# One unused 4-byte tile among the constants: every tile that grows from the bottom of SBUF moves up by 32 bytes

## The chip, the core and the metric

The kernel runs on one core of a Trainium2 chip. The metric is the device time of one execution in microseconds, as the median of several runs. The core has a matrix engine (TensorE, PE in the profile), three engines for elementwise work (VectorE or DVE, ScalarE or ACT, GpSimd or POOL) and a queue that issues transfers (SyncE, SP). Tiles live in SBUF, 128 partitions with a row of bytes each; an address here is the offset in that row. PE takes two operands from SBUF, the weights (stationary, loaded first) and the moving operand (streamed through), and writes its sums to PSUM.

## What is computed

A decoder trunk of two layers on 1024 tokens with 1024 channels, all in float32:

```python
for i in range(DEPTH):                       # DEPTH = 2
    mod = c_act @ ada_w[i] + ada_b[i]
    sh1, sc1, g1, sh2, sc2, g2 = [m[:, None, :] for m in jnp.split(mod, 6, axis=-1)]
    h = _rmsnorm(x, norm1_g[i]) * (1.0 + sc1) + sh1
    if i % N_MIXERS == 0:
        y = _dsa_mixer(h, positions, ...)    # indexer, top 256 keys, attention, w_out
    else:
        y = _short_conv_mixer(h, ...)        # conv_w_in, 3-tap convolution, conv_w_out
    x = x + g1 * y
    h = _rmsnorm(x, norm2_g[i]) * (1.0 + sc2) + sh2
    x = x + g2 * _swiglu(h, ffn_w_gate[i], ffn_w_up[i], ffn_w_down[i])   # hidden 2816
```

## The kernel before

**How products are formed.** Every large product is split in three: an operand x becomes hi = x rounded to the matrix engine's fp32r format and lo = x - hi, and `mm3` (line 510) issues three matmuls, hi x hi, hi x lo, lo x hi, into one PSUM bank. `split` (line 506) makes hi with ScalarE (a cast, or a copy on VectorE) and lo with VectorE. The call is `mm(ps, weights, moving)`: the second argument is the stationary operand, the third the moving one, 128 rows by 512 tokens in most of the program.

**Stages.** Norm and projections of the attention (to about 300 us), indexer and attention (to about 660 us), then the part that class `Tail` writes: FFN of layer 0 in `Pair` objects (lines 1772 to 1845), its down projection in `down_pairs` (line 1548), the convolution layer, again in `Pair` objects, its output product in `down` (line 1506), FFN and down projection of layer 1. A `Pair` and `down_pairs` use Strassen's scheme (Winograd's form): seven products in place of eight, and sums on VectorE around them.

**Who reads what.** In a `Pair` the weights come from the ring `whi`/`wlo` (four buffers each, `unit` at line 528) and the moving operands are the resident tiles `h11`, `h21`, `h22`, `t1` to `t4` (line 1405). In `down_pairs` five of the seven products move the tile `ph11` and two (`m2`, `m4`, lines 1659 and 1666) move buffers of the `whi`/`wlo` ring; the weights come from the ring in all seven. In `down` the first half of the tokens moves ring buffers, the second half the resident tiles `rh22` and `rt1`. The attention's projections move `hhi`/`hlo`. The profile leaves the numbers out of names: `h` stands for h11, h21 and h22, `t` for t1 to t4, `ph` for ph11 and ph21, `rt` and `rh` for the tiles that take the same places later.

**Where tiles lie.** Pools are stacks. Those without a side grow from the bottom of SBUF (constants, keys, the attention's buffers, and in the tail x, h, t and the small rings); those with `side="right"` grow down from the top (the weight ring, the raw loads, the attention's residents). Each tile's size is rounded up to 32 bytes. The constants are opened first and stay for the whole program, so everything on the left lies on top of them.

**What sets the order.** All instructions are recorded in `Plan` and emitted in an order that a list scheduler finds from priorities and a table of costs (line 207 on); a tile's address plays no part in it. A tile that no instruction uses is an allocation and nothing else.

Of the kernel before, what the change touches and what calls it, by code (L numbers as in the profile page):

```python
# [9 lines left out]
F32 = mybir.dt.float32  # L10
# [440 lines left out]
P = 128  # L451
# [35 lines left out]
class Trunk:  # L487
# [97 lines left out]
    def setup(self, c, positions, ada_b, n1, n2, conv_w, gq, gk, lg, lb, rope_c, arenas, kgb, freq):  # L585
        nc, cp = self.nc, self.cp
        self.ident = ident = cp.tile([P, P], F32, name="ident")
        nc.gpsimd.memset(ident, 1.0)
        nc.gpsimd.affine_select(ident, ident, pattern=[[-1, P]], compare_op=ALU.is_equal,
                                fill=0.0, base=0, channel_multiplier=1)  # L590
        self.blk4 = cp.tile([P, 4], F32, name="blk4")
        nc.vector.memset(self.blk4, 0.0)
        for i in range(4):
            nc.vector.memset(self.blk4[32 * i:32 * i + 32, i:i + 1], 1.0)
        rc = arenas[0].part_of(0)[0:9, P:2 * P]
        for r0, n, v in ((0, 8, c.rearrange("o (k p) -> (o k) p", p=P)), (8, 1, rope_c)):
            nc.scalar.dma_start(rc[r0:r0 + n, :], v)
        pv = self.ps("sm")
        nc.tensor.transpose(pv[:, 0:9], rc, ident[:9, :9])
        self.cact = cp.tile([P, 8], F32, name="cact")  # L600
        nc.scalar.activation(self.cact, pv[:, 0:8], AF.Silu)
        nc.vector.tensor_copy(freq, pv[:, 8:9])
        self.plan.pri = 1.0
        rows, rowb = arenas[0].part_of(1)[:, 0:P], arenas[1].part_of(0)[0:96, 0:P]
        nc.vector.memset(rows, 0.0)
        for r0, n, v in ((R_N1, 16, n1.rearrange("l (k p) -> (l k) p", p=P)),
                         (R_N2, 16, n2.rearrange("l (k p) -> (l k) p", p=P)),
                         (R_CW, 24, conv_w.rearrange("o w (k p) -> (o w k) p", p=P))):
            nc.sync.dma_start(rows.part_of((1, r0))[r0:r0 + n, :], v)
        nc.sync.dma_start(rowb, ada_b.rearrange("l (k p) -> (l k) p", p=P))  # L610
        g = arenas[1].part_of(96)[96:98, 0:HD]
        for r, v in enumerate((gq, gk)):
            nc.sync.dma_start(g[r:r + 1], v)
        for i, r in enumerate(R_G):
            nc.vector.tensor_copy(
                rows.part_of((1, r))[r:r + 2].rearrange("p (r q) -> p r q", q=32),
                g[:, 32 * i:32 * i + 32].unsqueeze(1).to_broadcast([2, 4, 32]))
        self.vec = vec = cp.tile([P, P], F32, name="vec")
        pv = self.ps("sm")
        read = [1] + [(1, r) for r in (R_N1, R_N2, R_CW, *R_G)]  # L620
        nc.tensor.transpose(pv[:, 0:P], rows.part_of(read), ident)
        nc.vector.tensor_copy(vec, pv[:, 0:P])
        self.adab = cp.tile([P, 96], F32, name="adab")
        pb = self.ps("sm")
        nc.tensor.transpose(pb[:, 0:96], rowb, ident[:96, :96])
        nc.vector.tensor_copy(self.adab, pb[:, 0:96])
        self.plan.pri = 25.0
        self.kgb = kgb.rearrange("p (a d) -> p a d", d=HD)
        for i, v in enumerate((lg, lb)):
            nc.sync.dma_start(self.kgb.part_of(i)[:, i], v.to_broadcast([P, HD]))  # L630
        mod = cp.tile([P, 2, 6, 8], F32, name="mod")
        self.mod = [[mod.part_of((i, j))[:, i, j] for j in range(6)] for i in range(2)]
        aff = cp.tile([P, 2, 2, 8], F32, name="aff")
        self.aff = [[aff.part_of((i, j))[:, i, j] for j in range(2)] for i in range(2)]
# [160 lines left out]
class Attention:  # L795
# [41 lines left out]


    def first_norm(self, x, positions, setup):
        tk, nc, plan, sp = self.tk, self.nc, self.plan, self.pj  # L840
        self.C, self.S = (self.hp.tile([P, T], F32, name=v) for v in "CS")
        plan.pri = 0.0
        setup((self.C, self.S))
        xt = self.kp.tile([P, 2, KT, HW], F32, name="xt", tag="karena")
        xT = [lambda d, i=i: xt.part_of((i, d))[:, i, d] for i in range(NH)]
# [1030 lines left out]
```

## Time and profile before

| | us |
|---|---|
| median of 3 runs | 2329.6 |
| lowest and highest | 2327.48, 2330.25 |
| the profiled execution, device time | 2336.01 |
| its span, first to last instruction | 2334.2 |
| mean granted clock of TensorE | 0.984 |

The page gives per engine the time in which it was busy, its share of the span and its instructions. A matmul's own length in a row (some 390 ns for 512 columns) holds its way through the array and overlaps the next one; the pace of the engine is the distance between two starts, so it is read from start times, from chain pieces ("us, what, xcount") or from counts in a window. In the views by line all of the kernel's work has line 244, because one function emits it; the tile names tell the work apart. In a table of windows each row has the window, its length, and for PE, PEld (weight loads), DVE, ACT, POOL the busy us and (xcount), then the granted clock, the busy share of the DMA engines and GB/s.

### The profile page before, as it was taken

The page shows a single profiled execution, that of the slowest core. Times are in us where ns is not written, and L with a number is a line of the kernel's source. Part 1 is how long each engine was busy: PE and PEld are TensorE (multiplying, and loading weights), DVE is VectorE, ACT ScalarE, POOL GpSimd, SP SyncE. Part 2 cuts the span into 40 slices and gives each one's busy share as a digit, 9 for nine tenths or more (in the row PEclk, how much of TensorE's full clock was granted, in tenths as well). Part 3 has the DMA queues.
Part 4 walks back from the last instruction along what each step waited for, and adds up shares of the span by engine and source line. Part 5 has one row for each costly group of instructions (what it writes and reads, how often), then busy time and mean ns, then how long its engine had stood idle before and what let it go on. Part 6 is the DMA issues. An engine that isn't in the chain of part 4 may idle for free.

```text
span 2334.2 us, 32524 instructions
## 1 busy us (share of the span) xinstructions
PE 2252.7 (97%) x11435; PEld 1777.3 (76%) x11435; DVE 1916.6 (82%) x3851; ACT 1125.7 (48%) x2140; POOL 4.6 (0%) x19
## 2 busy tenths in 40 slices
PE   4999999999999989999999999999999999999999
PEld 3657875766798868888888877777888788888887
DVE  7879999687689898878787999886898976768874
ACT  5476899756755323333444662224553333334444
POOL 0000000000000000000000000000000000000000
PEclk6999999999999999999999999999999999999999
DMA  9324233443344655544983354334446432339724
GB/s 308 112 64 95 87 108 106 130 129 103 113 142 143 197 194 163 177 132 160 348 314 104 100 144 122 118 108 154 119 125 198 150 117 86 122 126 384 283 82 135
DMA packets 334189, 356.34 MB, mean 153 GB/s; under 512 B 18089, under 2 KB 218826, under 8 KB 334026
## 3 DMA queue, kind: packets, MB, share of 16 engines
q1 hardware_dynamic: 333816, 354.14, 47.1%
q8 instruction: 89, 1.46, 0.3%
q14 instruction: 74, 0.61, 0.1%
q10 hardware_dynamic: 210, 0.14, 0.0%
HBM read 282.64 MB, written 71.57 MB: 152 GB/s over the span
## 4 chain that ended last, share of the span: by engine, by line
PE 72%; DVE 12%; DMA 5%; ACT 4%; issue 2%; SPq 0%; ACTq 0%; POOLq 0%; DVEq 0%
PE ps_g L244 42%; PE ps_mm L244 22%; PE ps_sm L244 5%; DVE s L244 2%; DVE u L244 2%; DMA raw<-in_conv_w_in_dram 2%; DVE wlo L244 2%; PE ps_L L244 2%; DMA adaw<-in_ada_w_dram 2%; PE ps_o L244 2%; DVE p L244 1%; ACT p L244 1%; DVE sc L244 1%; ACT junk L244 1%; DVE adacc L244 1%
## 5 line engine op out<-in xcount | busy, mean ns | idle before, releaser
L244 ACT CAST whi<-raw 128x512 fp32r<-128x512 f32 (+1 forms) x301 | 184.5, 619 | 417.4 <-PE ps_g L244 159.6
L244 PE MATMUL ps_g<-t,whi 128*128 128x512 f32 x1184 | 373.6, 397 | 1.8 <-DVE whi L244 1.8
L244 ACT CAST whi<-s 128x512 fp32r<-128x512 f32 x276 | 171.1, 621 | 358.3 <-PE ps_g L244 136.0
L244 PE MATMUL ps_g<-h,whi 128*128 128x512 f32 x1056 | 332.7, 396 | 0.1
L244 DVE TENSOR_TENSOR wlo<-raw,whi 128x512 fp32r<-128x512 f32 (+1 forms) x314 | 214.3, 687 | 89.1 <-ACT whi L244 88.0
L244 PEld LDWEIGHTS ps_g<-t,whi 128*128 128x128 f32 x1184 | 222.3, 188 | 56.3 <-DVE whi L244 2.6
L244 PE MATMUL ps_g<-t,wlo 128*128 128x512 f32 x592 | 235.1, 397 | 2.7 <-DVE wlo L244 2.7
L244 PEld LDWEIGHTS ps_g<-h,whi 128*128 128x128 f32 x1056 | 197.5, 188 | 47.9 <-ACT whi L244 0.5
L244 PE MATMUL ps_g<-h,wlo 128*128 128x512 f32 x528 | 209.0, 396 | 0.4 <-DVE wlo L244 0.4
L244 DVE TENSOR_TENSOR wlo<-s,whi 128x512 fp32r<-128x512 f32 x276 | 189.3, 688 | 21.8 <-ACT whi L244 21.5
L244 PE MATMUL ps_mm<-t,whi 128*128 128x512 f32 x608 | 191.7, 396 | 1.7 <-ACT whi L244 1.7
L244 PE MATMUL ps_g<-ph,whi 128*128 128x512 f32 x572 | 180.3, 395 | 0.0
L244 PEld LDWEIGHTS ps_mm<-t,whi 128*128 128x128 f32 x608 | 113.8, 188 | 30.0 <-ACT whi L244 2.6
L244 PEld LDWEIGHTS ps_g<-t,wlo 128*128 128x128 f32 x592 | 111.4, 188 | 32.4 <-DVE wlo L244 5.3
L244 PEld LDWEIGHTS ps_g<-ph,whi 128*128 128x128 f32 x572 | 107.3, 188 | 26.2
L244 ACT ACTIVATE p<-p,nm,qsc 128x256 f32<-128x256 f32 (+7 forms) x128 | 112.5, 883 | 22.1 <-DVE nm L244 17.0
L244 PE MATMUL ps_mm<-t,wlo 128*128 128x512 f32 x304 | 120.3, 396 | 0.3 <-DVE wlo L244 0.3
L244 DVE SCALAR_TENSOR_TENSOR adacc<-adaw,cact,adacc 128x512 f32<-128x512 f32 x140 | 104.8, 749 | 16.8 <-DMA adaw<-in_ada_w_dram 15.8
L244 PEld LDWEIGHTS ps_g<-h,wlo 128*128 128x128 f32 x528 | 99.0, 188 | 25.1 <-DVE wlo L244 1.2
L244 ACT ACTIVATE junk<-sc,bs 128x896 bf16<-128x896 f32 (+3 forms) x124 | 109.6, 884 | 16.4 <-DVE bs L244 13.1
L244 DVE CUSTOM_DVE_ANT_0 p<-ps_L,bias 128x512 f32<-128x512 f32 (+3 forms) x192 | 100.0, 552 | 20.5 <-PE ps_mm L244 10.9
L244 DVE TENSOR_TENSOR u<-u 128x512 f32<-128x512 f32 x170 | 114.8, 688 | 1.8 <-ACT u L244 0.8
(339 smaller groups left out, 4825.1 us busy)
## 6 DMA issues: line engine op xcount, KB each, us to landing
adaw<-in_ada_w_dram SPq DMA_DIRECT2D x160, 256.0 KB
ph<-in_ffn_w_down_dram SPq DMA_DIRECT2D x66, 512.0 KB
raw<-in_ffn_w_gate_dram SPq DMA_DIRECT2D x54, 512.0 KB
raw<-in_ffn_w_up_dram SPq DMA_DIRECT2D x54, 512.0 KB
raw<-in_conv_w_in_dram SPq DMA_DIRECT2D x34, 512.0 KB
raw<-in_ffn_w_down_dram SPq DMA_DIRECT2D x44, 256.0 KB
ph<-in_ffn_w_down_dram SPq DMA_DIRECT2D x44, 256.0 KB
raw<-in_attn_w_in_dram SPq DMA_DIRECT2D x18, 512.0 KB
```

What stands on the lines that cost most here:

```text
L244: f(*[a.get() if isinstance(a, Ref) else a for a in args], **{k: a.get() if isinstance(a, Ref) else a for k, a in kw.items()})
```

## The change

One line in `Trunk.setup`, behind the identity matrix:

```diff
         nc.gpsimd.affine_select(ident, ident, pattern=[[-1, P]], compare_op=ALU.is_equal,
                                 fill=0.0, base=0, channel_multiplier=1)
+        cp.tile([P, 1], F32, name="lead")
         self.blk4 = cp.tile([P, 4], F32, name="blk4")
```

The tile `lead` takes 4 bytes a partition, rounded up to 32, and nothing reads or writes it. The instructions of each engine, their order, their semaphores and the values that they wait for stay as they were; what differs is the addresses inside them. All left tiles behind `ident` move up by 32 bytes, right tiles stay:

| tile | side | address before | after | mod 64 before | after |
|---|---|---|---|---|---|
| ident | left | 5248 | 5248 | 0 | 0 |
| karena, later x (xr) | left | 7232 | 7264 | 0 | 32 |
| p (attention), 4 buffers | left | 40096 + 4096 k | 40128 + 4096 k | 32 | 0 |
| pf (attention), 7 buffers | left | 56800 + 2048 k | 56832 + 2048 k | 32 | 0 |
| h11, later ph11 | left | 52736 | 52768 | 0 | 32 |
| h21, later ph21 (raw loads) | left | 69120 | 69152 | 0 | 32 |
| h22, later rh22 | left | 85504 | 85536 | 0 | 32 |
| t1 to t4, later rt1 to rt4 | left | 101888 + 16384 k | 101920 + 16384 k | 0 | 32 |
| s (sums of the tail), 4 buffers | left | 196448 + 2048 k | 196480 + 2048 k | 32 | 0 |
| hhi, hlo (attention) | right | 74976 + 16384 k | same | 32 | 32 |
| raw, 2 buffers | right | 204768 + 4096 k | same | 32 | 32 |
| whi, 4 buffers | right | 212960 + 2048 k | same | 32 | 32 |
| wlo, 4 buffers | right | 221152 + 2048 k | same | 32 | 32 |

Rows of the h, t, ph, rh and rt tiles are cut into pieces of 2048 bytes, one for each matmul's moving operand, so each of these begins at the same remainder as its tile. Weights are cut from the ring in steps of 512 bytes (128 columns).

## Prediction

> **What bounds the kernel now.** I read the page first: the busy shares, then the chain that ended last.
>
> ```profile
> span 2334.2 us, 32524 instructions
> ...
> PE 2252.7 (97%) x11435; PEld 1777.3 (76%) x11435; DVE 1916.6 (82%) x3851; ACT 1125.7 (48%) x2140; POOL 4.6 (0%) x19
> ...
> PE 72%; DVE 12%; DMA 5%; ACT 4%; issue 2%; SPq 0%; ACTq 0%; POOLq 0%; DVEq 0%
> ```
>
> TensorE (PE) is busy 97% of the span and holds 72% of the chain. A busy PE is not by itself a bound, so the list of waits comes next: who stands still for whom (total us, times, longest us).
>
> ```profile
> ACT whi L244 <- PE ps_g L244: 304.5, 178, 3.3
> ...
> ACT whi L244 <- DMA raw<-in_conv_w_in_dram: 52.5, 15, 5.1
> ```
>
> The engine that prepares the weights waits 304.5 us for PE to give buffers back, and 52.5 us for the transfers of the convolution's input weights. The DMA queue's own list says the same one step further back:
>
> ```profile
> SPq L244 <- DVE wlo L244: 682.1, 195, 30.2
> ```
>
> Loads are held back 682.1 us because the splits before them, which themselves wait for PE, have not freed the raw buffers. So in most of the program PE sets the pace, with prepared weights queued ahead of it. The third view is the split by stage:
>
> ```profile
> 0.00:40.00 40.00, 19.43 (x82) 14.54 (x83) 26.87 (x63) 21.68 (x35) 1.76 (x13) 0.69 0.89 322
> 1100.00:1190.00 90.00, 90.00 (x387) 72.35 (x386) 66.53 (x107) 38.53 (x66) 0.00 (x0) 1.00 0.89 323
> 1286.00:1306.00 20.00, 20.00 (x90) 16.57 (x89) 18.18 (x30) 9.31 (x17) 0.00 (x0) 1.00 0.27 92
> 1850.00:2050.00 200.00, 200.00 (x859) 160.70 (x858) 148.01 (x237) 65.03 (x109) 0.00 (x0) 1.00 0.36 116
> 2100.00:2200.00 100.00, 100.00 (x431) 80.33 (x430) 81.42 (x131) 43.06 (x75) 0.00 (x0) 1.00 0.98 362
> 1400.00:1520.00 120.00, 118.93 (x510) 94.95 (x509) 109.11 (x192) 31.11 (x52) 0.00 (x0) 1.00 0.40 117
> 800.00:900.00 100.00, 93.74 (x391) 72.21 (x390) 89.58 (x151) 27.45 (x47) 0.00 (x0) 0.98 0.63 204
> ```
>
> From 1850 to 2050 us PE runs 859 matmuls without a gap at the full granted clock (1.00) and VectorE (DVE) is busy 74%. The time there is matmuls times spacing. From 800 to 900 us and from 1400 to 1520 us PE has gaps while DVE is busy 90 and 91%: there PE is not alone at the limit.
>
> **Two spacings.** The change alters no instruction, only addresses. So the question is whether any duration in the trace depends on an address. One does. The timeline of PE (start, length, tiles, count), at a place where two kinds of matmul alternate:
>
> ```profile
> 1275.23 0.63 PE L244 MATMUL ps_g<-ph,whi 128*128 128x512 f32 x2
> ...
> 1278.03 0.39 PE L244 MATMUL ps_mm<-whi 128*128 128x512 f32 x1
> ...
> 1279.42 0.39 PE L244 MATMUL ps_mm<-whi 128*128 128x512 f32 x1
> ...
> 1280.78 0.63 PE L244 MATMUL ps_g<-ph,whi 128*128 128x512 f32 x2
> ...
> 1283.58 0.40 PE L244 MATMUL ps_mm<-whi 128*128 128x512 f32 x1
> ```
>
> Between 1275.23 and 1278.03, and again between 1280.78 and 1283.58, stand twelve matmuls that read their moving operand (the 128x512 one) from `ph`: 2.80 us for 12, 233.3 ns each. Between 1279.42 and 1280.78 stand six that read it from `whi` or `wlo`: 1.36 us for 6, 226.7 ns each. Both kinds take their weights from the same ring, in the same shape, in the same microseconds at the same clock. What differs is where the moving operand lies: `ph` begins at 52736, a multiple of 64, and the `whi` and `wlo` buffers begin 32 past one. Long stretches say the same: in the chain, three to a row and twelve to a row,
>
> ```profile
> 1290.58 0.68 PE ps_mm L244 x3
> ```
>
> ```profile
> 2003.65 2.80 PE ps_mm L244 x12
> ```
>
> 0.68 us for 3 (226.7 ns) from `whi`, 2.80 us for 12 (233.3 ns) from `t`. The region doesn't explain it: `t` lies where `hhi` lay during the projections. How long is the step in bytes? The output projection's matmuls are 256 columns wide and also read right tiles:
>
> ```profile
> 663.46 5.76 PE ps_sm L244 x48
> ```
>
> That is 120.0 ns each, so 256 further columns cost 226.7 - 120.0 = 106.7 ns, 0.417 ns a column. The step of 6.67 ns is 16 columns' time, 64 bytes of the moving row. That makes 64 the first guess for the period in the address.
>
> **The change part by part.** It adds an allocation and no instruction; order, semaphores and waits stay. It shifts every left tile by 32 bytes: `h`, `t`, `ph`, `rh` and `rt`, now at multiples of 64, land 32 past one, like `whi`. The weights don't move.
>
> *The matmuls that gain.* 4,704 in the pairs (44 in the two FFNs and 12 in the convolution, each 7 products of 4 x 3 matmuls), 1,320 in `down_pairs` (5 of its 7 products, 11 steps, 12 matmuls, 2 layers) and 192 in the second half of `down` (8 x 8 x 3): 6,216 of 128x512. The two largest groups of the list by line and tile:
>
> ```profile
> L244 PE MATMUL ps_g<-t,whi 128*128 128x512 f32 x1184 | 373.6, 397 | 1.8 <-DVE whi L244 1.8
> L244 PE MATMUL ps_g<-h,whi 128*128 128x512 f32 x1056 | 332.7, 396 | 0.1
> ```
>
> 6,216 x 6.67 ns = 41.4 us if PE paces all of them.
>
> *What the next bound takes back.* From 1400 to 1520 us (x510) I count nothing as gained, because transfers and DVE end the waits there: 510 x 6.67 = 3.4 us lost. From 800 to 900 us (x391; up to 2.6 us) I count half, 1.3 us lost. Elsewhere the queue of prepared weights covers it: a DVE busy 148 us in 200 still has 46 us to spare when the 200 become 194.
>
> *Plain f32 work of the attention.* `pf` goes from 32 past a multiple of 64 to 0, against `vst` weights that stay; `karena` the other way.
>
> ```profile
> L244 PE MATMUL ps_L<-karena,qst 64*128 64x512 f32 (+3 forms) x384 | 87.6, 541 | 7.4 <-DVE mx L244 7.4
> ...
> L244 PE MATMUL ps_o<-pf,vst 128*64 128x128 f32 x1152 | 77.5, 279 | 2.2 <-ACT on L244 1.9 <-DVE bs L244 0.2
> ```
>
> Nothing shows these at both offsets. Bounds by the same step, for 576 pairs of `pf` and 192 pairs of `karena`: 3.8 us lost or gained, 1.3 us lost or gained. I take 0, since no row favours either sign.
>
> *ScalarE (ACT) and DVE.* The same operation where its tiles are right (32 past) and left (multiples of 64):
>
> ```profile
> L244 ACT CAST whi<-raw 128x512 fp32r<-128x512 f32 (+1 forms) x301 | 184.5, 619 | 417.4 <-PE ps_g L244 159.6 <-PE ps_mm L244 127.1 <-DMA raw<-in_conv_w_in_dram 52.5
> ...
> L244 ACT CAST ph<-rt 128x512 fp32r<-128x512 f32 x78 | 48.3, 619 | 72.4 <-PE ps_g L244 36.7 <-PE ps_sm L244 25.7 <-issue 3.9
> ```
>
> ```profile
> L244 DVE TENSOR_TENSOR wlo<-raw,whi 128x512 fp32r<-128x512 f32 (+1 forms) x314 | 214.3, 687 | 89.1 <-ACT whi L244 88.0
> ...
> L244 DVE TENSOR_TENSOR ph<-rt,ph 128x512 fp32r<-128x512 f32 x80 | 54.8, 687 | 13.0 <-ACT ph L244 12.9
> ```
>
> 619 against 619 ns, 687 against 687 ns: nothing.
>
> *Transfers.* Left targets lose their alignment. From 0 to 40 us all bulk loads go to right tiles (32 past): 322 GB/s at a busy share of 0.89, 362 per full share. From 1100 to 1190 us much goes to left tiles at multiples of 64: 323 at 0.89, 363; from 2100 to 2200 us 362 at 0.98, 369. That is 0 to 2%, and in the two stretches together (190 us), if they became bound by it, 0 to 3.8 us lost. I take 0, because PE ran there without a gap (x387 in 90 us, x431 in 100 us).
>
> **The sum**, against the profiled execution's 2336.0 us (span 2334.2): 41.4 - 3.4 - 1.3 = 36.7 us, so 2299.3 us. That execution lies 0.27% above the median of the runs, 2329.6; scaled by 0.9973 the forecast is **2293 us**. Its own range: at best everything is kept and the attention's two bounds are gains, 46.5 us, 2283; at worst both thin stretches keep nothing and all bounds are losses, 41.4 - 3.4 - 2.6 - 5.1 - 3.8 = 26.5 us, 2303.
>
> **Against the page.** The spacings above are 226.7 and 233.3 ns. The Trainium skill's page "TensorE: Matmul & The Clock Gate" (Back-to-back issue gap) gives N/2.4 + 2.5 ns for a warm matmul, 216 ns for N = 512, with no term for an address, and says under "Step-by-step: what each phase is for" that loading the next weights does not take read bandwidth from the running matmul. By that rule the sum is 0. The trace disagrees with it by 11 and 17 ns, and with itself between the two addresses.
>
> **The rivals.**
>
> 1. *No change, 2330 us (0.10).* Fast operands lie not only at 32 mod 64: all begin at 224 mod 256, as do the full-width weights they meet. The left ones go from 0 to 32 mod 256. If what counts is the distance between moving operand and weights in 128 or 256 bytes, 32 may be as slow as 0; then 6,216 x 0 is saved. For it: no row shows residue 32. Against it: the 64-byte step. The skill's rule above gives the same time.
>
> 2. *Half-way, 2315 us (0.07).* After an interruption a `whi` matmul does not settle at once:
>
> ```profile
> 2288.88 0.60 PE L244 MATMUL ps_sm<-ident,xr 128*128 128x128 f32 x4
> ...
> 2289.55 0.39 PE L244 MATMUL ps_mm<-wlo,whi 128*128 128x512 f32 x1
> ...
> 2291.86 0.39 PE L244 MATMUL ps_g<-whi,wlo 128*128 128x512 f32 x1
> ```
>
> Ten spacings in 2.31 us, 231 ns. If left operands never settle, the saving is 2.3 ns x 6,216 = 14.3 us: 2321.7, scaled 2315.
>
> 3. *Slower, 2371 us (0.08).* The mechanism that costs 64 bytes' time at one distance costs another 64 bytes' time at the new one: 240 ns. Place: the same 6,216 matmuls; price + 41.4 us, scaled 2371. It decides as soon as the spacing in the FFNs exceeds 233.3 ns, since PE is gapless there and every ns costs 6.2 us. For it: residue 32 is unseen. Against it: no 128x512 group settles above 233.3.
>
> **How the numbers follow.** Forecast 0.75, half-way 0.07, no change 0.10, slower 0.08. A measurement of this kernel tells 0.2% (4.7 us) from no change, so forecast and half-way are faster (0.82), the first rival is the same (0.10), the third slower (0.08). The range takes in the forecast's 2283 to 2303 and the half-way case, which the two thin stretches (901 x 2.3 ns = 2.1 us) can bring from 2315 to 2318: 2283 to 2318. It leaves out 0.18.
>
> **What would show it.** Right: between 1850 and 2050 us some 884 matmuls instead of 859, chain pieces of 12 in 2.72 us, the `whi` stretches unchanged, the FFN stages shorter by 2.9%, the stages before 650 us within a few us, the waits at the convolution longer. Wrong: pieces of 12 still at 2.80 us (rival 1), near 2.77 (rival 2), at 2.88 (rival 3); or 2.72 with the gain lost in new waits for transfers or DVE.

## The result, and the profile after

The changed kernel takes 2312.29 us (median; 2308.23 to 2317.03), beside 2330.25 us before: a ratio of 0.9921 with an interval of 0.9897 to 0.9946, so 18 us less. The forecast was 2293 us, 37 us less than the median it started from. The direction holds, and a little under half of the forecast gain is there. The stated range, 2283 to 2318 us, holds too, but by luck: the forecast's own range was 2283 to 2303, and 2312 lies inside only because the half-way rival's time was taken in.

The page of the changed kernel, for the profiled execution, the slowest of the five (2317.03 us):

```profile
span 2314.6 us, 32524 instructions
...
PE 2232.5 (96%) x11435; PEld 1783.6 (77%) x11435; DVE 1911.9 (83%) x3851; ACT 1126.1 (49%) x2140; POOL 4.6 (0%) x19
...
PE 73%; DVE 11%; DMA 5%; ACT 3%; issue 2%; SPq 0%; ACTq 0%; POOLq 0%; DVEq 0%
```

TensorE (PE) still holds 73% of the chain, and its busy time fell by 20.2 us, about as much as the span (19.6). The waits for PE shrank, as they must when it gives buffers back sooner (304.5 to 291.9 us, and 682.1 to 665.5 us in the DMA queue behind it); the one for the convolution's input weights grew a little (52.5 to 54.2 us):

```profile
ACT whi L244 <- PE ps_g L244: 291.9, 175, 3.3
...
ACT whi L244 <- DMA raw<-in_conv_w_in_dram: 54.2, 15, 5.2
```

```profile
SPq L244 <- DVE wlo L244: 665.5, 195, 30.2
```

The split by stage of the changed kernel, in four of the windows shown of before (us, then busy time and instructions of PE, PEld, DVE, ACT and POOL, then granted clock, DMA share, GB/s):

```profile
1100.00:1190.00 90.00, 90.00 (x395) 73.76 (x394) 68.45 (x109) 40.24 (x69) 0.00 (x0) 1.00 0.94 344
1850.00:2050.00 200.00, 200.00 (x875) 164.13 (x874) 147.39 (x235) 65.36 (x110) 0.00 (x0) 1.00 0.32 102
2100.00:2200.00 100.00, 99.99 (x436) 81.47 (x435) 84.13 (x135) 44.57 (x76) 0.00 (x0) 1.00 0.91 329
1400.00:1520.00 120.00, 117.22 (x506) 94.17 (x505) 108.94 (x190) 30.13 (x50) 0.00 (x0) 1.00 0.42 123
```

From 1850 to 2050 us PE runs 875 matmuls where it ran 859; the forecast said 884. The chain there consists of pieces like the first below. The second is from a stretch at 1280 us where the moving operand is `whi` or `wlo`:

```profile
1854.05 2.75 PE ps_mm L244 x12
```

```profile
1280.02 0.68 PE ps_g L244 x3
```

Twelve matmuls that move a left tile take 2.75 us, about 229 ns each: neither the 2.80 of before nor the 2.72 of the forecast. Three that move a right tile still take 0.68 us. **A third spacing has appeared.**

The clearest measure takes the same matmuls in both kernels. All programs here issue the same matmuls in the same order, so they can be counted through. Matmuls 9,800 to 10,400 are 600 of the second FFN, all with a left moving operand. Before:

```profile
1956.13:2096.13 140.00, 140.00 (x602) 112.48 (x601) 100.77 (x160) 46.04 (x78) 0.00 (x0) 1.00 0.33 108
```

After:

```profile
1942.01:2079.35 137.34, 137.34 (x602) 112.68 (x600) 100.80 (x161) 45.98 (x78) 0.00 (x0) 1.00 0.34 111
```

140.00 us for 600 is 233.3 ns; 137.34 is 228.9 ns. (The view counts the two matmuls at the edges too, hence x602.) The saving is 4.43 ns a matmul, where the forecast put 6.67.

### The profile page after: what moved, and what is told of

It is laid out like the page before. It is cut to its first block, busy times and chain, and to the rows that moved or that the text cites. A ratio compares the mean times of both kernels' runs of the same rounds, so it can differ in the third digit from the quotient of the medians.

```text
span 2314.6 us, 32524 instructions
## 1 busy us (share of the span) xinstructions
PE 2232.5 (96%) x11435; PEld 1783.6 (77%) x11435; DVE 1911.9 (83%) x3851; ACT 1126.1 (49%) x2140; POOL 4.6 (0%) x19
## 4 chain that ended last, share of the span: by engine, by line
PE 73%; DVE 11%; DMA 5%; ACT 3%; issue 2%; SPq 0%; ACTq 0%; POOLq 0%; DVEq 0%
PE ps_g L244 42%; PE ps_mm L244 23%; PE ps_sm L244 5%; DMA raw<-in_conv_w_in_dram 2%; DVE s L244 2%; PE ps_L L244 2%; PE ps_o L244 2%; DVE u L244 2%; DVE wlo L244 1%; DVE p L244 1%; ACT p L244 1%; DVE sc L244 1%; DMA adaw<-in_ada_w_dram 1%; DVE adacc L244 1%; DVE v L244 1%
## 5 line engine op out<-in xcount | busy, mean ns | idle before, releaser
L244 PE MATMUL ps_g<-t,whi 128*128 128x512 f32 x1184 | 368.5, 393 | 2.6 <-DVE whi L244 2.6
L244 DVE TENSOR_TENSOR wlo<-s,whi 128x512 fp32r<-128x512 f32 x276 | 188.6, 686 | 17.6 <-ACT whi L244 15.2
L244 PEld LDWEIGHTS ps_mm<-t,whi 128*128 128x128 f32 x608 | 114.0, 188 | 26.9 <-ACT whi L244 2.5
L244 PEld LDWEIGHTS ps_g<-h,wlo 128*128 128x128 f32 x528 | 99.1, 188 | 24.3 <-DVE wlo L244 2.3
```

The costliest lines, as they stand in the source:

```text
L244: f(*[a.get() if isinstance(a, Ref) else a for a in args], **{k: a.get() if isinstance(a, Ref) else a for k, a in kw.items()})
```

## The experiments

The tiles that matter, in bytes modulo 256, before the change: left moving operands (`h`, `t`, `ph`, `rh`, `rt`) at 0, full-width weights and `whi`/`wlo` at 224. "Distance" below is moving operand minus weights, modulo 256: 32 before, 64 after the change, 0 where `whi` meets weights of its own ring.

### One pool moved: 96 and 64 bytes up

```
-        cp.tile([P, 1], F32, name="lead")
+        cp.tile([P, 24], F32, name="lead")
```

and the same with 16 for 64 bytes. Written ahead of them:

> Left tiles 96 bytes higher than before instead of 32: the moving operands of the pairs lie at 96 mod 128, the same residue as whi and as all full-width weights. Theory A (the spacing goes by the distance between moving operand and weights, period 128): distance 0, 226.7 ns, as for whi. Theory B (it goes by the moving operand's own residue, period 128): 226.7 ns too. Theory C (period 64 as forecast, and the missing 2.4 ns come from something else about left tiles): 229.1 ns, as with 32 bytes. A and B: 6,216 x 6.6 = 41 us less 3 to 5 us in the thin stretches, about 2294 us beside a before of 2330; C: about 2312.

> Left tiles 64 bytes higher: moving operands at 64 mod 128, weights at 96 mod 128. Theory A: distance 96 mod 128, a value no run shows; if the spacing is symmetric in the distance, 233.3 ns as at 32, else anything from 226.7 up. Theory B: residue 64, also unseen. Theory C (period 64): 233.3 ns and no change, 2330 us. Not a test between A and B by itself: it fills in the fourth value.

Measured: 96 bytes up 2329.88 us, ratio 0.9982 (0.997 to 0.9994); 64 bytes up 2333.36 us, ratio 0.9997 (0.9983 to 1.0012). The window 1850 to 2050 us with 96 bytes up:

```profile
1850.00:2050.00 200.00, 200.00 (x862) 162.22 (x862) 147.82 (x237) 65.37 (x110) 0.00 (x0) 1.00 0.33 105
```

With 64 bytes up:

```profile
1850.00:2050.00 200.00, 200.00 (x859) 160.93 (x858) 147.94 (x237) 65.38 (x110) 0.00 (x0) 1.00 0.36 114
```

862 and 859 matmuls: 232.5 and 233.3 ns. So 96 bytes up gains next to nothing, although the moving operand then has the residue of `whi` modulo 128. All three theories that were written down for it fail there: A and B wanted 226.7 ns, C 229. The 233.3 ns at 64 bytes are what C gave, and A if the distance counts symmetrically.

### The other pools moved

All right tiles 32 bytes down, left ones as before; then left ones 32 up and right ones 64 down (`[P, 8]` for the lead, `[P, 16]` for the edge):

```
+        edge = Pool(plan, "edge", side="right")
+        edge.tile([P, 8], F32, name="edge")
+        plan.open(edge, ctx)
         plan.open(tk.wp, ctx)
```

> Left tiles as before, all right tiles 32 bytes lower: weights, whi and hhi at 64 mod 128, left moving operands at 0. Theory A: left ones at distance 64, 229.1 ns, as in the changed kernel; right ones (whi, hhi) keep distance 0 and 226.7 ns; about 2311 us. Theory B: left ones keep residue 0 and 233.3 ns; right ones take the value of residue 64 (left64 shows it); 2330 us or above. Theory C: left ones 233.3 ns, right ones 233.3 ns; above 2330 us.

> Left tiles 32 bytes higher as in the change, all right tiles 64 bytes lower: moving operands and weights all at 32 mod 128. Theory A: distance 0 everywhere, 226.7 ns for left and right ones, about 2294 us. Theory B: residue 32 everywhere, 229.1 ns for left and right ones, about 2312 us or somewhat above. Theory C: 229.1 left, 226.7 right, 2312 us.

Right tiles 32 down: 2311.45 us, ratio 0.9892 (0.9868 to 0.9916).

```profile
1850.00:2050.00 200.00, 200.00 (x876) 164.17 (x875) 147.77 (x236) 64.75 (x108) 0.00 (x0) 1.00 0.33 105
```

Both moved: 2327.5 us, ratio 0.9966 (0.9952 to 0.998).

```profile
1850.00:2050.00 200.00, 200.00 (x863) 162.20 (x862) 147.79 (x237) 65.42 (x110) 0.00 (x0) 1.00 0.33 105
```

The first is the decisive run. No left tile moved, and the spacing still fell to that of the change: so the moving operand's own residue doesn't decide. The second answers to 96 bytes up: other residues, the same distance of 128, nearly the same count (863, 862); here too all three theories miss, with 226.7 and 229 ns forecast and 232.6 measured. Two pairs of kernels, (0, 192) with (32, 224) and (32, 160) with (96, 224), agree by distance alone. Theory A thus had the right quantity and the wrong period: in 128 bytes, 96 up has distance 0 and should be fast; in 256 it has 128. With period 256 only distance 0 is known to be fast (`whi` on its own ring), and the left tiles can be put there by going down.

### Distance 0: 32 bytes down

```
-        self.vec = vec = cp.tile([P, P], F32, name="vec")
+        self.vec = vec = cp.tile([P, 120], F32, name="vec")
...
-        nc.vector.tensor_copy(vec, pv[:, 0:P])
+        nc.vector.tensor_copy(vec, pv[:, 0:120])
```

> The tile vec of the constants is cut from 128 to 120 columns (columns 98 to 127 are never read), so all left tiles behind it lie 32 bytes lower than before: moving operands of the pairs at 224 mod 256, like all full-width weights. Theory D (the spacing goes by the distance moving operand minus weights, period 256: 0 gives 226.7, 32 gives 233.3, 64 gives 229.0, 96 gives 233.3, 128 gives 232.5 ns): distance 0, 226.7 ns, 6,216 x 6.6 = 41 us less some 4 us in the thin stretches, ratio about 0.984. Theory E (distance with period 128, and left tiles never get below 229 ns): 232.5 ns as with 96 bytes up, ratio about 0.998.

Measured: 2304.44 us, ratio 0.988 (0.9865 to 0.9896), the fastest of all. The same window, and the 600 matmuls counted through:

```profile
1850.00:2050.00 200.00, 200.00 (x884) 165.58 (x884) 150.63 (x240) 66.14 (x111) 0.00 (x0) 1.00 0.34 111
...
1933.01:2069.01 136.00, 136.00 (x602) 112.61 (x600) 101.03 (x161) 45.98 (x78) 0.00 (x0) 1.00 0.34 112
```

884 matmuls, the number the forecast had given for the change itself; 136.00 us for 600, 226.7 ns. Theory D holds for the spacing, E falls: nothing in left tiles keeps them from the speed of `whi`. The time did not follow all the way: 28.8 us against the 37 that D gave. That is taken up below.

### The spacing by itself

Matmuls alone, with the offsets of the moving row and of the weights as the only variables:

```
for i in range(n):
    ps = pp.tile([P, 512], F32, name="ps")
    a, c = m // 4 + 512 * (i // 4 % 4), w // 4 + 128 * (i % 4)
    nc.tensor.matmul(ps, lhsT=wt[:, c:c + 128], rhs=mv[:, a:a + 512], start=True, stop=True)
...
for turn in range(2):
    for w in (0, 32, 96):
        for m in (range(0, 256, 16) if turn == 0 else reversed(range(0, 256, 16))):
            group(m, w, 32)
```

> Only matmuls of 128x512 f32r, nothing beside them (the whole trunk is left out, the output is a copy of x): 32 for each of 16 offsets of the moving row (0 to 240 in steps of 16 bytes) against weights at offsets 0, 32 and 96, all of it twice in opposite order. Theory D: the spacing is a function of the distance alone, the same for the three weights' offsets: 226.7 ns at 0, 229 at 64, 232 to 233.5 at 32, 96 and 128; 160, 192 and 224 mirror 96, 64 and 32 if it is symmetric; steps of 16 unseen. Rival F (the waits come from the traffic of VectorE and ScalarE, which the address only lets through): with both idle every offset gives the same spacing, 227 ns or less. Rival G (own residues of moving operand and weights count apart): values that differ between the three weights' offsets at equal distance.

Nothing else ran there but a few operations at the start and the copy of x, which is over by 40 us, while the first 200 matmuls warm up:

```profile
PE 761.2 (98%) x3272; PEld 616.4 (79%) x3272; DVE 1.6 (0%) x2; POOL 0.2 (0%) x4
```

Mean interval of start to start in ns, worked out from the trace's 62 to 64 intervals of each cell (the kernels' column: all intervals of warm left matmuls in the trace of the kernel with that distance):

```
distance   weights at 0   at 32   at 96   in the kernels
   0          227.3       227.6   227.9   226.9 (32 down)
  16          231.8       231.6   231.8
  32          233.3       233.4   233.3   233.3 (before)
  48          231.6       233.2   231.6
  64          229.1       229.0   229.1   229.0 (change; right 32 down)
  80          231.1       231.2   231.1
  96          233.6       233.4   233.6   233.3 (64 up)
 112          230.9       231.7   230.9
 128          232.7       233.2   232.7   232.5, 232.6 (96 up; both)
 144          233.2       233.3   232.9
 160          234.1       234.3   234.0
 176          233.3       233.2   233.3
 192          233.3       233.3   233.1
 208          234.7       232.3   234.5
 224          233.0       233.3   233.3
 240          231.9       230.1   230.1
```

With VectorE and ScalarE idle the spacing still goes by the distance, so it is no traffic of theirs (rival F falls). The weights' own offset hardly counts: the columns agree within 0.6 ns, but for 0.8 at 112 and 1.6 to 2.4 at 48, 208 and 240. The numbers of the kernels come back to within 1 ns. It is not symmetric: 64 gives 229, 192 gives 233. Only 0 and 64 are good, among the steps of 32.

The means hide one thing. Each cell was run twice, in opposite order, and where the columns part, the two turns part. Means of each turn's 31 intervals, in ns:

```
distance  turn     weights at 0   at 32   at 96
  48      first       233.1       233.1   233.2
          second      230.0       233.4   230.0
 208      first       234.7       234.7   234.5
          second      234.5       230.0   234.5
 240      first       226.9       226.9   226.9
          second      236.6       233.4   233.4
```

In the first turn the three columns agree within 0.3 ns at every distance but 0 (226.7, 227.9, 227.9), so rival G falls. But the same two addresses can settle at different spacings, 226.9 or 233 and more at distance 240, in stretches that differ only in what ran before them. The distance is the main thing, and not the whole rule.

The second such kernel alternates distances within a group, and takes other widths and types:

```
group(F32R, 512, [144], [0, 144], 64)
group(F32R, 512, [0, 144], [0], 64)
for t, n in ((F32R, 256), (BF16, 512), (F32, 512)):
    for m in range(0, 256, 32):
        group(t, n, [m], [0])
```

> Only matmuls again (the whole trunk is left out, the output is a copy of x). First 128x512 f32r with weights alternating between distance 0 and 144, then with the moving row alternating between the same two and the weights fixed. If the wait arises while a moving row runs beside the load of the next weights: with alternating weights the interval after a matmul whose successor's weights lie at distance 144 is the long one (233 ns), the other 227, and the mean is 230; if it arises against the weights already in place, the long interval is the other one; a mean off 230 says that neighbours act together. Then 128x256 f32r, 128x512 bf16 and 128x512 f32, each at distances 0 to 224 in steps of 32: if it is a matter of bytes read, the 256 wide show about half the step in ns or the same 2 to 7 ns, bf16 (half the bytes in the same columns) shows less or none, f32 shows a step too; if it is a fixed price for each weight load, all three show about the same 2 to 7 ns.

With weights alternating, the interval is 234.8 ns after a matmul whose own weights are at distance 0 and whose successor's are at 144, and 231.7 ns the other way round (one interval of 631 ns left out). With the moving row alternating, it is 234.5 ns after the row at distance 0 and 233.9 ns after the row at 144. In the first group the long interval goes with the successor's weights, as if the load beside the moving row counted; in the second the row at distance 0 should then be followed by the short one, and it isn't. The means, 233.2 and 234.2, are not 230 either. So neighbours act together, no simple reading of the expectation holds, and the cause isn't settled. By type: 128x512 bf16 takes 215.8 to 216.2 ns at all eight distances. 128x512 f32 shows two records of 429.2 ns each a matmul, at all eight. Of these only f32r depends on the distance, and 256 columns wide it does so differently: 119.6 ns at 0, 114.0 at 192, between 117.4 and 119.7 elsewhere.

### The change again, and its twin

The change was timed twice more, unaltered, the second time beside the kernel with right tiles 32 down, which has the same distance of 64.

> The change itself, timed again beside the other kernels. If its 8 us of loss in the first 170 us of the profiled run were luck of the clock grants: 6,216 x 4.3 = 26.7 us less about 2 us in the thin stretches, ratio 0.989 to 0.990. If that loss belongs to the change: 18 us, ratio 0.992, and the same half-clock windows at 77 and 135 us in the profile.

> The change once more, beside the next one on the same chip: same spacing expected in both (distance 64, 229.0 ns). If only the spacing decides, the two ratios agree within their intervals, at 0.990 to 0.993, and the half-clock window at 76 us is luck: it can be missing here. If shifting left tiles has a price of its own, the window at 76 us shows a third time and this kernel is slower than the other by 3 us or more.

> Right tiles 32 bytes lower, left tiles as before, once more: 229.0 ns. If only the spacing decides: the same ratio as the change beside it, 0.990 to 0.993. If shifting left tiles has a price of its own: 0.989, 3 us or more below the change, and no half-clock window at 76 us.

Measured: the change 2315.03 us, ratio 0.9935 (0.9916 to 0.9954), and 2310.96 us, ratio 0.9909 (0.9885 to 0.9933); its twin 2313.17 us, ratio 0.9908 (0.9888 to 0.9929). Beside each other the two are equal, as the spacing alone wants. The first of these repeats came out as the second answer had it, at 0.9935, and its profile shows the half-clock window (a stretch with a granted clock of 0.5) at 76 us again; but at 135 us it has 3 us of half clock for 17, and at 210 us it is only 1 us behind. The other repeat lacks the window at 76 us. So the first 200 us are read from the profiles. Before,

```profile
60.00:120.00 60.00, 57.10 (x307) 41.68 (x306) 50.92 (x107) 32.11 (x61) 0.77 (x2) 1.00 0.35 106
120.00:200.00 80.00, 72.93 (x340) 46.30 (x339) 66.55 (x149) 54.16 (x128) 2.11 (x4) 0.96 0.16 47
```

the change, first profile,

```profile
60.00:120.00 60.00, 57.13 (x295) 42.11 (x294) 48.28 (x99) 29.45 (x54) 0.77 (x2) 0.94 0.32 97
120.00:200.00 80.00, 72.70 (x308) 45.22 (x307) 61.41 (x134) 52.58 (x128) 1.51 (x4) 0.89 0.16 46
```

and the change, third timing:

```profile
60.00:120.00 60.00, 57.88 (x303) 41.89 (x302) 50.86 (x106) 32.13 (x61) 0.77 (x2) 0.97 0.35 106
120.00:200.00 80.00, 73.09 (x343) 46.61 (x342) 67.34 (x151) 54.85 (x129) 2.11 (x4) 0.96 0.17 48
```

Granted clocks of 0.94 and 0.89 cost the first profiled execution some 8 us by 200 us into the span; the same program is granted 0.97 and 0.96 in the third, and at matmul 2,000 (399 us) it stands level with before to 0.04 us. That loss changes from execution to execution of one program; it is one reason why a single profile of this kernel carries an error of several us.

The third profile shows something else, in the down projection of layer 0. Before:

```profile
1160.00:1260.00 100.00, 100.00 (x430) 80.38 (x429) 85.57 (x138) 41.49 (x72) 0.00 (x0) 1.00 0.74 263
```

the change, first profile:

```profile
1160.00:1260.00 100.00, 100.00 (x439) 82.04 (x438) 84.90 (x136) 42.13 (x74) 0.00 (x0) 1.00 0.71 252
```

and the change, third timing:

```profile
1160.00:1260.00 100.00, 100.00 (x431) 80.98 (x430) 79.62 (x128) 41.10 (x71) 0.00 (x0) 1.00 0.64 222
```

Behind one interval of 259 ns at 1148 us, 499 matmuls of the change follow each other at 233.3 ns up to 1265 us, without a gap and at the full granted clock; in its first two profiles the same matmuls take 228.9. The program and the addresses are the same. So at distance 64, too, a stretch can settle at another spacing, here that of before; it cost this execution 499 x 4.42 ns = 2.2 us. The prediction's own rows have a short case: the six `whi` matmuls from 1278.03 to 1279.42, right behind those of `ph`, take 231.7 ns each, the next six 226.7. What decides which spacing a stretch takes was not tested.

## Where the prediction held, and where it failed

**PE sets the pace: right.** In gapless stages the time fell by matmuls times spacing. The 4.43 ns are themselves worked out from such a stretch, so the test is the one with distance 0: 600 x 6.67 ns, from the prediction's rows, is 4.00 us, exactly 140.00 - 136.00.

**An address sets the spacing: right.** Two spacings were read correctly from the alternating stretch, and the region was rightly excluded: left tiles at distance 0 reach 226.7 ns.

**"That makes 64 the first guess for the period in the address": wrong, and the step that failed.** From it followed that left tiles "land 32 past one, like `whi`" and gain 6.67 ns. The runs show that the distance to the weights, modulo 256 bytes, sets the spacing in nearly all stretches (`hhi` and `hlo`, 347 to 539 times 256 bytes from the first `whi` buffer, settle at 227 ns like `whi`), and the change moves it from 32 to 64: 4.43 ns. The term of 41.4 us should have been 6,216 x 4.43 = 27.5 us. Those 13.9 us are most of the shortfall of 19 (36.7 forecast, 18.0 measured). The 64 bytes came from dividing 6.67 ns by the time of one column; the third spacing, 229 ns, fits no such step, so the agreement of 16 columns with a round number proved nothing. The first rival had the right quantity in its sentence on "the distance between moving operand and weights in 128 or 256 bytes", and noted that residue 32 was unseen; but it took 32 to be as slow as 0, and got 0.10.

**What the next bound takes back: right in kind, too small.** The convolution's stretch, matmuls 7,200 to 8,000 with 792 left ones. Before:

```profile
1347.55:1536.65 189.10, 186.59 (x802) 148.79 (x801) 173.92 (x303) 67.36 (x114) 0.00 (x0) 1.00 0.43 126
```

After:

```profile
1340.29:1528.92 188.63, 184.22 (x802) 148.78 (x800) 173.58 (x303) 67.02 (x114) 0.00 (x0) 1.00 0.43 126
```

32 bytes down:

```profile
1330.00:1520.23 190.23, 184.81 (x801) 149.63 (x800) 174.08 (x304) 67.12 (x114) 0.00 (x0) 0.99 0.43 126
```

Less PE time, no shorter stretch: VectorE's 174 us and the transfers hold it, as forecast, but over 792 matmuls and not 510. The trace of before could have told: in this stretch PE has 39% of its chain, transfers of the convolution's input weights 22% and VectorE some 32%. At 4.43 ns it loses 792 x 4.43 = 3.5 us less the 0.47 it kept, 3.0 us. The second and third profiles of the change have 190.95 and 190.29 us there, 5.4 and 4.7 us lost. With distance 0 it loses 792 x 6.67 ns + 1.13 us = 6.4 us, some 1.6 of them to a half-clock window at 1338 us. With distance 0 transfers come in as well, from 1100 to 1190 us:

```profile
1100.00:1190.00 90.00, 88.88 (x391) 72.96 (x390) 69.31 (x112) 39.18 (x67) 0.00 (x0) 1.00 1.03 376
```

PE stands still once, for 1.1 us, at a DMA share of 1.03, in a window where it ran without a gap before; transfers hold a third of the chain in this window, which was PE alone before. So even with 226.7 ns the forecast of 36.7 us would have been some 8 us too high: 28.8 were measured.

**The rest of the sum.** With the right spacing the forecast's own steps give 27.5 less 510 x 4.43 = 2.3 less 0.9 for 800 to 900 us: 24.3 us. The three timings gave 18.0, 18.2 and 23.0 us (differences of medians: 2330.25 - 2312.29, 2333.20 - 2315.03, 2334.00 - 2310.96). From matmul 4,200 on (662 us before), where all left matmuls lie, the profiles behind them save 24.4, 19.7 and 17.6 us of the 27.5. Part of the difference has a place: the convolution's stretch (3.0, 5.4 and 4.7 us lost), the third profile's 2.2 us at 233.3 ns, and half-clock windows of 3.4 us, at 851 and 1342 us in the second (the later one inside the convolution's stretch) and at 850 and 1815 in the third (before has one at 875, the first none). In such a window these matmuls start 427 ns apart, so each costs up to 1.6 us. How the rest of the 1 to 6 us by which the timings fall short of 24.3 divides between clock and waits in the thin stretches isn't settled.

**Zeros that held.** ScalarE and VectorE on tiles that moved and tiles that didn't, after:

```profile
L244 ACT CAST whi<-raw 128x512 fp32r<-128x512 f32 (+1 forms) x301 | 184.5, 619 | 412.8 <-PE ps_g L244 155.5
...
L244 DVE TENSOR_TENSOR ph<-rt,ph 128x512 fp32r<-128x512 f32 x80 | 54.7, 686 | 10.2 <-ACT ph L244 9.9
```

619 and 686 ns, as before to 1 ns. Transfers: 344 GB/s at a share of 0.94 and 329 at 0.91 are 366 and 362 per full share, where it was 363 and 369. The plain f32 matmuls: those of `pf` against `vst` went from distance 0 to 32 and take 78.0 us for 77.5,

```profile
L244 PE MATMUL ps_o<-pf,vst 128*64 128x128 f32 x1152 | 78.0, 280 | 2.0 <-ACT on L244 1.8
```

and by themselves f32 matmuls of 128x512 don't depend on the distance at all, so the bounds of 3.8 and 1.3 us could have been zeros. Not explained: between 400 and 520 us the profiled executions of the change are 2 to 4 us shorter than that of before, in jumps where PE waits; the matmul stretches there keep their lengths. Those of the other shifted kernels are shorter there too, by 0.6 to 4.1 us, so it may belong to the one profiled execution of before.

**The rule that was weighed.** The Trainium skill's "TensorE: Matmul & The Clock Gate" (Back-to-back issue gap) gives 216 ns for N = 512 as the gap of an isolated matmul, and about 131 ns as a sustained figure. The trace agrees with the first for bf16, 215.8 ns; the second shows in no run here. For f32r the best is 226.7 ns. The Trainium skill's page "SBUF — State Buffer" (SBUF: two separate sides) states that PE never waits on anyone at its ports. The f32r numbers, 227 to 234 ns by distance with the other engines idle, would fit a wait between PE's own two reads; no run here shows the ports, and the cause stays open.

**The rivals.** The half-way rival had nearly the time (2315 us), by luck: it let the matmuls never settle, while they settle at 229 ns. "No change" and "slower" fall; 233 ns is about the worst at any step of 32 (160 gives 234).

## What to carry to other kernels

In a kernel that PE bounds with f32r matmuls, compare the chain's spacing between groups of one shape: a difference of a few ns at equal clock may be an address, and 32 bytes in the layout can be worth 1%. Don't guess the period from one pair of values: a few hundred matmuls alone, over offsets of 16 bytes, give the table in one run. Run them in more than one order, and read the orders apart before you take a mean. Then aim for the best entry (here distance 0 modulo 256 for 512 columns), and cost what the next bound takes back stage by stage: of 41 us in the matmuls, 29 reached the time.

## What was not expected of the hardware

- The spacing of 128x512 f32r matmuls goes, in nearly all stretches, by the distance between moving row and weights modulo 256 bytes: 227 ns at 0, 229 at 64, 232.5 to 234 at the other steps of 32. With 256 columns the best is another distance: 114.0 ns at 192, 119.6 at 0.
- It can settle at another spacing at the same addresses: 499 matmuls of the change at 233.3 ns in one execution and 228.9 in two others, and alone, at distance 240, 226.9 ns in one order and 233.4 to 236.6 in the other.
- bf16 (215.8 to 216.2 ns) and f32 (429.2 ns a record) of 512 columns don't depend on it.
- After the first 60 us, half-clock windows of 3 to 17 us lie partly at other places in each execution of the same program; between two of them this made 8 us by 210 us into the span.
